# The first shift vector by halves of its columns, worked in between the steps of the first projection

## The chip, the cores and the metric

One Trainium2 chip, of which this kernel uses one core: TensorE (matrix products), VectorE, ScalarE, GpSimd (POOL in the profile) and SyncE (SP), which here does nothing but issue transfers. The metric is device microseconds for one execution, as a median of three runs.

## The reference, cut to what matters

One transformer layer over 256 tokens of 1024 features, batch 1. A condition vector c gives six vectors of 1024, and the first two of them modulate the normalised input ahead of one wide projection:

```
mod = silu(c) @ w_ada + b_ada          # six vectors: sh1, sc1, g1, sh2, sc2, g2
u   = normalize(x) * (1 + sc1) + sh1
proj = u @ w_in                        # 1024 -> 2560: x, y, q, k, v, 512 columns each
mix = [rmsnorm(rg_lru(conv(x)) * gelu(y)), rmsnorm(attention(q, k, v))] @ w_out
x   = layernorm(alpha * x + g1 * mix)
out = layernorm(alpha * x + g2 * experts(modulate(x, sh2, sc2)))   # 32 experts, top 2
```

The change touches only sh1, "the first shift vector", and its way into the first 512 columns (x) of the projection. All weights are float32.

## The kernel before

**Order of work.** The program is written out by hand: each engine executes its instructions in the order of the source, and semaphores hold an instruction until what it reads is there. So an instruction that waits also holds everything behind it on its engine. All large weights are brought by transfers that SP issues in program order (L229 in the helper `load`, two transfers of 1 MB each); a transfer into a buffer is issued once the last reader of the buffer is done.

**Modulation.** The two vectors come from `ada`, the columns of w_ada. `cd` holds silu(c), each value repeated 32 times. `scale_mm(a)` (L361) multiplies it with 512 columns of w_ada for half a of the scale vector: 32 products, each of 128 columns, four of them side by side in the four column strips of the array; float32 takes two instructions for one product, so 64 in the profile. VectorE copies the result out (L368). `scale_end` (L371) turns the row into columns with a small product (L373) and adds the bias on VectorE (L375) into `mod1[:, 1]`. `vec_cols(0)` (L377) does the same for the whole shift vector at once: products of 256 columns (L381), a copy (L384), two small products (L387), and at L465 the bias into `mod1[:, 0]`.

**First projection.** `proj_T` (L419) computes 512 columns of the projection in eight steps k, 12 products (L430) of 256 columns a step. Weights and activations are split into a high and a low float32r part, and three of the four part products are summed. `ahead` (L402) splits the weights: ScalarE writes the high part (L407, or L410 with the scale vector multiplied in), VectorE the low one (L408, L411), into four buffers `w`. `after` is called behind a step's products, `mid` behind the first six.

**The shift in the x part.** The x part runs before the shift vector is known: its weights are multiplied by the scale vector, its activations are the plain normalised input, and the contribution of the shift is one row vector, `shift @ w_in[:, 0:512]`, that is added later as a bias. For it VectorE spreads `mod1[:, 0]` into `shd` (L467), TensorE multiplies `shd` with the x weights (L481, eight products of 512 columns, 16 instructions), ScalarE copies the result (L503), TensorE turns it into columns (L507). All other parts take fully modulated activations, which `u_part(k)` (L469) makes for slice k: ScalarE writes the high part (L470), VectorE (k even) or GpSimd (k odd) overwrites the plain activations (L471), and VectorE subtracts for the low part (L473).

**What stands where.** The x part is L454, with `gate_constants` (L337) behind step 6: a chain of some thirty tiny operations, most of them on GpSimd, each waiting for the one before. Then: issue of the y weights (L455) and of `pkb`; `vec_cols(0)` (L458); the split of the first y weights (L459); issue of the q weights, of `wgt`, of a row of biases behind a GpSimd fill of `brows` (L462), and of the next part of w_ada (L464); the shift vector (L465 to L467); `u_part` 0 and 1; the 16 instructions of L481; issue of the k weights, of T and of another part of w_ada. Then the y part (L515), in whose steps 0 to 5 the `u_part` 2 to 7 stand. Behind it comes one instruction group of `ada_mm` (L578), the q part, and so on through attention, output projection, router and experts.

Of the kernel before, what the change touches and what calls it, by code (L numbers as in the profile page):

```python
# [10 lines left out]
F32 = mybir.dt.float32  # L11
# [4 lines left out]
AF = mybir.ActivationFunctionType  # L16
OP = mybir.AluOpType
# [5 lines left out]
H, DH = 8, 64  # L23
NE, DE = 32, 256
KD = D // 128
# [122 lines left out]
def layer(ctx: ExitStack, tc: tile.TileContext, at_a, at_b, x, w_ada, b_ada, w_in, w_out, w1, w3, w2,  # L148
          pack_a, pack_b, w_gate, rb, ln, out, dbg=None):
    nc = tc.nc  # L150
    te, ve, se, ge, sy = nc.tensor, nc.vector, nc.scalar, nc.gpsimd, nc.sync
# [42 lines left out]
    def bank(pool=None):  # L194
        turn[0] += 1
        return (pool or (psx, psp)[turn[0] % 2]).tile([128, 512], F32, name="b")

    def abank():
        return psa.tile([128, 512], F32, name="a")
# [8 lines left out]
    def A(name):  # L208
        o, w = at_a[name]
        return pka[:, o:o + w]  # L210
# [21 lines left out]
    def load_vec(v, q, s):  # L232
        return load(s, ada[:, 4 * q:4 * q + 4, v * D:(v + 1) * D])

    def load_ada(g, q, s):
        return load(s, ada[:, 2 * q:2 * q + 2, g * 2048:(g + 1) * 2048])

    def load_win(j, s):
        return load(s, win[:, :, j * 512:(j + 1) * 512])
# [13 lines left out]
    for a in range(2):  # L253
        V1[1, a] = load(a, ada[:, :, D + a * 512:D + a * 512 + 512])
        sy.dma_start(W["x"][:, 4 * a:4 * a + 4], win[:, 4 * a:4 * a + 4, 0:512])
    V1[0, 0] = load_vec(0, 0, 3)
    V1[0, 1] = load_vec(0, 1, 4)
    ident = A("ident")

    negh = cst.tile([128, 2], F32, name="negh")  # L260
# [76 lines left out]
    def gate_constants():  # L337

        ge.tensor_scalar(hb, P("ba", 0, 8), 0.5, None, op0=OP.mult)
        lam = P("lam", 0, 4)  # L340
        a_, w_, s_, q_, acc_, r_ = [sp[:, i] for i in range(6)]
        ve.tensor_scalar(a_, lam, -1.0, None, op0=OP.mult)
        ve.tensor_tensor(a_, a_, lam, op=OP.max)
        se.activation(w_, a_, AF.Exp, scale=-1.0)
        ge.tensor_scalar(s_, w_, 2.0, None, op0=OP.add)
        ve.reciprocal(s_, s_)
        ge.tensor_mul(s_, s_, w_)
        ge.tensor_mul(q_, s_, s_)
        ge.memset(acc_, 1.0 / 19)
        for n in range(8, -1, -1):  # L350
            ge.tensor_mul(acc_, acc_, q_)
            ge.tensor_scalar(acc_, acc_, 1.0 / (2 * n + 1), None, op0=OP.add)
        ge.tensor_mul(acc_, acc_, s_)
        ve.tensor_scalar(r_, lam, -1.0, 0.0, op0=OP.mult, op1=OP.max)
        ge.tensor_scalar(acc_, acc_, 2.0, None, op0=OP.mult)
        ge.tensor_add(r_, r_, acc_)
        ge.tensor_scalar(cs[:, 0], r_, -0.5 * LRU_C, None, op0=OP.mult)
        ge.tensor_scalar(cs[:, 1], r_, 0.5 * LRU_C, None, op0=OP.mult)


    def scale_mm(a):  # L361
        pa = abank()
        for k in range(KD):
            for j in range(4):
                te.matmul(pa[32 * j:32 * j + 32, 0:128], cd[:, k], V1[1, a][:, k, j * 128:(j + 1) * 128], start=(k == 0),
                          stop=(k == KD - 1), skip_group_check=True, tile_position=(0, 32 * j))
        r = tmp.tile([128, 256], F32, name="row", bufs=1)[:, 0:128]
        ve.tensor_copy(r, pa[:, 0:128])  # L368
        return r

    def scale_end(a, r):  # L371
        p = bank(psp)
        te.matmul(p[:, 0:4], r, sel4, start=True, stop=True)  # L373
        q = slice(4 * a, 4 * a + 4)
        ve.scalar_tensor_tensor(mod1[:, 1, q], p[:, 0:4], 1.0, A("bcol")[:, 8 + 4 * a:12 + 4 * a], op0=OP.add, op1=OP.add)  # L375

    def vec_cols(v):  # L377
        pa = abank()
        for k in range(KD):
            for j in range(4):  # L380
                te.matmul(pa[32 * j:32 * j + 32, 0:256], cd[:, k], V1[v, k // 4][:, k % 4, j * 256:(j + 1) * 256],  # L381
                          start=(k == 0), stop=(k == KD - 1), skip_group_check=True, tile_position=(0, 32 * j))
        r = tmp.tile([128, 256], F32, name="row", bufs=1)
        ve.tensor_copy(r, pa[:, 0:256])  # L384
        p = bank(psx)
        for s in range(2):
            te.matmul(p[:, s:8:2], r[:, s * 128:(s + 1) * 128], sel4, start=True, stop=True)  # L387
        return p[:, 0:8]

    mod1 = ch.tile([128, 2, 8], F32, name="mod1")  # L390
    for b in range(4):
        n_parts(b)
    scale_end(0, scale_mm(0))
    te.matmul(pv[:H, :384], rbt[:, 384:392], rbt[:, 0:384], start=True, stop=True)


# [2 lines left out]
    def rows_of(w, scale=None):  # L399
        units.extend((w, k, scale) for k in range(KD))  # L400
# [34 lines left out]

    rows_of(W["x"], mod1[:, 1])
    row = [None]

    def after_x(k):
        if k < 2:  # L440
            n_copy(2 * k)
            n_copy(2 * k + 1)
        if k == 1:
            bias_rows()
        if k == 2:
            row[0] = scale_mm(1)
        elif k == 6:
            gate_constants()

    def mid_x(k):  # L450
        if k == 3:
            scale_end(1, row[0])

    px = proj_T(0, psp, after_x, mid_x, lambda k: 4 if k < 4 else 8, (0, 4))  # L454
    W["y"] = load_win(1, 0)  # L455
    sy.dma_start(pkb, pack_b)
    rows_of(W["y"])
    p = vec_cols(0)  # L458
    ahead(9)  # L459
    W["q"] = load_win(2, 3)  # L460
    sy.dma_start(wgt, w_gate)
    ge.memset(brows[:, 0], 0.0)  # L462
    sy.dma_start(brows[0:128:32, 0], b_ada[4:8])
    AD[1, 0] = load_ada(1, 0, 1)  # L464
    ve.tensor_add(mod1[:, 0], p, A("bcol")[:, 0:8])  # L465
    shd = misc[:, 3072:3328].rearrange("p (k n) -> p k n", k=KD)
    ve.tensor_copy(shd, mod1[:, 0, :, None].to_broadcast([128, KD, 32]))  # L467

    def u_part(k):  # L469
        se.activation(ul[:, 0, k], nT[:, k], AF.Identity, scale=mod1[:, 1, k:k + 1], bias=mod1[:, 0, k:k + 1])  # L470
        (ge if k % 2 else ve).tensor_scalar(nT[:, k], nT[:, k], mod1[:, 1, k:k + 1], mod1[:, 0, k:k + 1], op0=OP.mult,  # L471
                                            op1=OP.add)
        ve.tensor_sub(ul[:, 1, k], nT[:, k], ul[:, 0, k])  # L473

    u_part(0)
    u_part(1)

    pb = bank(psx)
    for k in range(KD):
        j = k % 4  # L480
        te.matmul(pb[32 * j:32 * j + 32], shd[:, k], W["x"][:, k], start=(k < 4), stop=(k >= 4), skip_group_check=True,  # L481
                  tile_position=(0, 32 * j))
    W["k"] = load_win(3, 2)
    sy.dma_start(T, bass.AP(tensor=vrd.tensor, offset=vrd.offset, ap=[[1, 128], [384, H], [1, 256]]))
    AD[1, 1] = load_ada(1, 1, 4)
    rowx = brows[:, 1]
    xb = ch.tile([128, 4], F32, name="xb")
    xl, xc = t4(0), t4(1)
# [8 lines left out]
                                    op0=OP.mult, op1=OP.add)  # L497

    def after_y(k):
        if k < 6:  # L500
            u_part(k + 2)
        if k == 0:
            se.activation(rowx, pb, AF.Copy)  # L503
        elif k == 2:
            pb2 = bank(psp)
            for j in range(4):
                te.matmul(pb2[:, j:j + 1], rowx[:, j * 128:(j + 1) * 128], inv32, start=True, stop=True)  # L507
            ve.tensor_copy(xb, pb2[:, 0:4])
        elif k < 7 and k > 2:
            shift(k - 3)  # L510
        if k > 4:
            conv(k - 5)

    rows_of(W["q"])
    py = proj_T(8, psx, after_y)  # L515
    W["v"] = load_win(4, 0)
    gy = nx[:, 1].rearrange("p (m t) -> p m t", m=4)
    for b in range(2):
# [1217 lines left out]
```

## Time and profile before

| | |
|---|---|
| median of 3 runs | 307.26 us (307.08 to 308.35) |
| profiled execution | 307.51 us |
| span of its trace | 305.7 us |
| TensorE busy | 278.0 us, 91% |
| VectorE / ScalarE / GpSimd busy | 181.7 / 108.2 / 23.6 us |
| mean granted TensorE clock | 0.988 of full |
| bytes moved by transfers | 112.22 MB, mean 367 GB/s |

Times are microseconds from the start of the span. The profiled execution took 307.51 us, of which 1.81 us lie around the span. The page gives each engine's busy share in 40 slices, the clock granted to TensorE, and the busy share of the transfer engines; a busy TensorE is not TensorE at its peak, since matrix products overlap. "Chain" is the chain of work that ended last, followed back from the last instruction.

### The profile page before, as it was taken

What the parts mean: (1) busy time and instruction counts of PE and PEld (TensorE: products, weight loads), DVE (VectorE), ACT (ScalarE), POOL (GpSimd) and SP (SyncE); (2) the same over time, 40 slices, a digit from 0 to 9 for tenths busy, and PEclk for the clock granted to TensorE, in tenths of its full rate; (3) what the DMA queues carried; (4) which work ended last, traced back from release to release, by engine and by line L of the source; (5) the groups of instructions that cost most, each with busy time, mean ns of one, the idle gap of its engine ahead of it and who ended that gap; (6) DMA issues with size and microseconds to landing.
All of it is one profiled execution on the core that took longest, in us unless ns stands there. A gap on an engine that the chain in (4) does not pass through costs nothing.

```text
span 305.7 us, 6096 instructions
## 1 busy us (share of the span) xinstructions
PE 278.0 (91%) x2344; PEld 185.1 (61%) x2344; DVE 181.7 (59%) x442; ACT 108.2 (35%) x229; POOL 23.6 (8%) x62
## 2 busy tenths in 40 slices
PE   0699889999999999999988969999999999998980
PEld 0579649797957745457475656667546754664430
DVE  2675167937686796689698964264426343434281
ACT  1233068868937542043417341113111312121110
POOL 0100613000010000000110200000000000400000
PEclk9999979999999999999999999999999999999997
DMA  7999999999999699699969999999999999999404
GB/s 271 387 391 408 393 396 404 385 395 420 411 409 407 248 416 421 235 402 378 323 263 364 364 416 427 418 421 419 423 423 415 421 419 420 421 414 404 177 3 148
DMA packets 26163, 112.22 MB, mean 367 GB/s; under 512 B 2253, under 2 KB 3586, under 8 KB 17420
## 3 DMA queue, kind: packets, MB, share of 16 engines
q1 hardware_dynamic: 25712, 111.26, 91.7%
q10 hardware_dynamic: 348, 0.47, 0.4%
q8 instruction: 20, 0.33, 0.4%
q14 instruction: 19, 0.16, 0.2%
q0 software_dynamic: 64, 0.01, 0.0%
HBM read 110.51 MB, written 1.22 MB: 365 GB/s over the span
## 4 chain that ended last, share of the span: by engine, by line
PE 63%; DMA 13%; DVE 12%; SPq 6%; ACT 2%; issue 2%; DVEq 0%; ACTq 0%
PE m L1212 14%; PE b L430 12%; PE m L1350 8%; PE b L804 7%; DMA arena<-in_w 6%; DMA arena<-in_w_in 6%; SPq L229 4%; PE b L779 4%; PE m L1288 4%; PE acc L1311 3%; PE a L578 2%; PE a L590 2%; PE acc L1387 1%; PE b L481 1%; PE b L617 1%
## 5 line engine op out<-in xcount | busy, mean ns | idle before, releaser
L430 PEld LDWEIGHTS b<-ul,w 128*128 128x128 f32 x384 | 46.6, 192 | 5.0 <-ACT ul L470 1.6
L430 PE MATMUL b<-ul,w 128*128 128x256 f32 x384 | 48.4, 286 | 0.5 <-ACT w L410 0.5
L1212 PE MATMUL m<-arena,xg 128*64 128x256 f32 (+1 forms) x288 | 36.1, 380 | 1.0 <-DMA arena<-in_w 1.0
L408 DVE TENSOR_TENSOR w<-arena,w 128x512 fp32r<-128x512 f32 x32 | 21.9, 700 | 16.1 <-ACT w L407 16.1
L1350 PE MATMUL m<-arena,hT 128*32 128x512 f32 (+2 forms) x184 | 29.1, 596 | 1.6 <-ACT hT L1341 1.6
L804 PE MATMUL b<-arena,mT 128*128 128x512 f32 x64 | 29.0, 601 | 0.0
L1212 PEld LDWEIGHTS m<-arena,xg 128*64 128x64 f32 (+1 forms) x288 | 21.1, 125 | 9.9 <-DMA arena<-in_w 1.7
L407 ACT ACTIVATE w<-arena 128x512 fp32r<-128x512 f32 x32 | 19.5, 625 | 13.9 <-DMA arena<-in_w_in 7.1
L1212 PE MATMUL m<-fifth,xg 128*32 128x256 f32 (+1 forms) x96 | 21.5, 380 | 0.0
L1212 PE MATMUL m<-misc,xg 128*32 128x256 f32 (+1 forms) x160 | 21.4, 380 | 0.0
L1362 DVE SCALAR_TENSOR_TENSOR ys<-m,ws,g2b 128x256 f32<-128x256 f32 (+1 forms) x21 | 11.4, 570 | 16.0 <-PE m L1350 15.8
L1363 ACT ACTIVATE yh<-ys 128x256 fp32r<-128x256 f32 (+1 forms) x21 | 10.0, 488 | 27.0 <-DVE ys L1362 26.9
L1331 DVE TENSOR_TENSOR hh<-hh,m 128x256 f32<-128x256 f32 x7 | 3.0, 422 | 27.9 <-ACT hh L1330 27.9
L804 PEld LDWEIGHTS b<-arena,mT 128*128 128x128 f32 x64 | 11.6, 191 | 13.0 <-issue 12.7
L1350 PEld LDWEIGHTS m<-arena,hT 128*32 128x32 f32 (+2 forms) x184 | 8.6, 120 | 17.8 <-issue 12.7
L1330 ACT ACTIVATE hh<-m 128x256 f32<-128x256 f32 x7 | 2.7, 385 | 41.1 <-PE m L1212 41.1
L1288 PE MATMUL m<-oh,xb 128*128 128x256 f32 (+1 forms) x64 | 15.4, 281 | 1.3 <-DVE oh L1279 1.3
L1288 PE MATMUL m<-oh,xa 128*128 128x256 f32 (+1 forms) x64 | 15.4, 282 | 0.0
L1212 PEld LDWEIGHTS m<-misc,xg 128*32 128x32 f32 (+1 forms) x160 | 13.3, 126 | 1.6 <-issue 0.8
L1212 PE MATMUL m<-last,xg 128*32 128x256 f32 x64 | 14.2, 380 | 0.0
L728 ACT ACTIVATE s<-s,z 128x128 f32<-128x128 f32 (+1 forms) x16 | 7.1, 449 | 18.3 <-DVE z L726 18.3
L305 PE MATMUL b<-pka,nx 128*128 128x128 f32 x16 | 3.9, 428 | 10.3 <-DVE nx L303 10.3
(321 smaller groups left out, 501.2 us busy)
## 6 DMA issues: line engine op xcount, KB each, us to landing
arena<-in_w SPq DMA_DIRECT2D x41, 1024.0 KB, 11.9
arena<-in_w_ada SPq DMA_DIRECT2D x22, 1024.0 KB, 13.9
arena<-in_w_in SPq DMA_DIRECT2D x10, 1024.0 KB, 15.1
last<-in_w SPq DMA_DIRECT2D x6, 1024.0 KB, 12.2
misc<-in_w SPq DMA_DIRECT2D x6, 1024.0 KB, 13.3
fifth<-in_w SPq DMA_DIRECT2D x6, 1024.0 KB, 13.0
arena<-in_w_out SPq DMA_DIRECT2D x4, 1024.0 KB, 8.8
arena<-in_w SPq DMA_DIRECT2D x8, 512.0 KB, 12.7
```

The source lines that it names most:

```text
L229: sy.dma_start(t[:, q], src[:, q])
L407: se.activation(t[:, 0], w[:, k], AF.Copy)
L408: ve.tensor_sub(t[:, 1], w[:, k], t[:, 0])
L430: te.matmul(half(bs, m), t[:, a, m * 128:(m + 1) * 128], ul[:, b, k], start=(k + m % 2 + a + b == 0), stop=(k == KD - 1 and a == 1), skip_ ...
L779: te.matmul(pvv[i], ul[:, ua, k, i * 128:(i + 1) * 128], t[:, wa], start=(k + wa + ua == 0), stop=(k == KD - 1 and wa == 1))
L804: te.matmul(p, mT[:, k, i * 128:(i + 1) * 128], wo[k // 4][:, k % 4, h * 512:(h + 1) * 512], start=(m == 0), stop=(m == 3))
L1212: te.matmul(ph[o:o + w, a * 256:(a + 1) * 256], xs[:, k, o:o + w], place[q][0].rearrange("p (a k f) -> p a k f", a=2, k=KD)[:, a, k], star ...
L1288: te.matmul(q, nhl[i][:, a, k * 128:(k + 1) * 128], oh[:, i, :n], start=(a + i == 0), stop=(a + i == 2))
L1311: te.matmul(acc[i][h], G[:, i * 128:(i + 1) * 128], y[:, sl], start=False, stop=False, skip_group_check=True)
L1350: te.matmul(ps[h][o:o + w], hT[:, j, o:o + w], place[q][1][:, j * 1024 + h * 512:j * 1024 + (h + 1) * 512], start=(j == 0), stop=(j == 1), ...
L1362: ve.scalar_tensor_tensor(ys[:, o:o + q], p[:, o:o + q], ws, g2b[:, sl], op0=OP.mult, op1=OP.mult)
L1363: se.activation(yh[:, sl], ys[:, o:o + q], AF.Copy)
```

## The change

It loads the shift vector's columns of w_ada in two halves of 512 columns, as the scale vector's are, in place of two halves of the rows. `scale_mm` and `scale_end` become `col_mm(v, a)` and `col_end(v, a, r)` for both vectors, and `vec_cols` goes. The first half of the shift vector is worked in the x part: `col_mm(0, 0)` behind step 5, `col_end` and the spread into `shd` in the middle of step 6, `u_part` 0 and 1 behind step 6, 2 and 3 behind step 7. `gate_constants` moves from behind step 6 to behind step 4. The second half stands behind the x part: `col_mm(0, 1)`, then the first half of the shift's product (`shift_mm(0)`), then `col_end` and the spread. The second half of the product stands behind step 0 of the y part, with the issue of the k weights, T and the next w_ada part; `u_part` 4 to 7 stand behind the y steps 0 and 1. Issue of the q weights and what follows is written ahead of `col_mm(0, 1)`. In step 0 of the y part the products with the low weights come last.

```diff
-    V1[0, 0] = load_vec(0, 0, 3)
-    V1[0, 1] = load_vec(0, 1, 4)
+    for a in range(2):
+        V1[0, a] = load(3 + a, ada[:, :, a * 512:a * 512 + 512])
...
-    def scale_mm(a):
+    def col_mm(v, a):
...
-    def scale_end(a, r):
-        p = bank(psp)
+    def col_end(v, a, r):
+        p = bank(psx if v == 0 else psp)
         te.matmul(p[:, 0:4], r, sel4, start=True, stop=True)
         q = slice(4 * a, 4 * a + 4)
-        ve.scalar_tensor_tensor(mod1[:, 1, q], p[:, 0:4], 1.0, A("bcol")[:, 8 + 4 * a:12 + 4 * a], op0=OP.add, op1=OP.add)
+        ve.scalar_tensor_tensor(mod1[:, v, q], p[:, 0:4], float(v), A("bcol")[:, 8 * v + 4 * a:8 * v + 4 * a + 4], op0=OP.add,
+                                op1=OP.add)
...
+    def shift_cols(a):
+        q = slice(4 * a, 4 * a + 4)
+        ve.tensor_copy(shd[:, q], mod1[:, 0, q, None].to_broadcast([128, 4, 32]))
...
         if k == 2:
-            row[0] = scale_mm(1)
+            row[0] = col_mm(1, 1)
+        elif k == 4:
+            gate_constants()
+        elif k == 5:
+            row[0] = col_mm(0, 0)
         elif k == 6:
-            gate_constants()
+            u_part(0)
+            u_part(1)
+        elif k == 7:
+            u_part(2)
+            u_part(3)
 
     def mid_x(k):
         if k == 3:
-            scale_end(1, row[0])
+            col_end(1, 1, row[0])
+        elif k == 6:
+            col_end(0, 0, row[0])
+            shift_cols(0)
...
     W["y"] = load_win(1, 0)
     sy.dma_start(pkb, pack_b)
-    rows_of(W["y"])
-    p = vec_cols(0)
-    ahead(9)
     W["q"] = load_win(2, 3)
     sy.dma_start(wgt, w_gate)
     ge.memset(brows[:, 0], 0.0)
     sy.dma_start(brows[0:128:32, 0], b_ada[4:8])
     AD[1, 0] = load_ada(1, 0, 1)
-    ve.tensor_add(mod1[:, 0], p, A("bcol")[:, 0:8])
-    shd = misc[:, 3072:3328].rearrange("p (k n) -> p k n", k=KD)
-    ve.tensor_copy(shd, mod1[:, 0, :, None].to_broadcast([128, KD, 32]))
...
-    u_part(0)
-    u_part(1)
+    rows_of(W["y"])
+    rows_of(W["q"])
 
     pb = bank(psx)
-    for k in range(KD):
...
+    def shift_mm(a):
+        for j in range(4):
+            te.matmul(pb[32 * j:32 * j + 32], shd[:, 4 * a + j], W["x"][:, 4 * a + j], start=(a == 0), stop=(a == 1),
+                      skip_group_check=True, tile_position=(0, 32 * j))
+
+    r = col_mm(0, 1)
+    shift_mm(0)
+    col_end(0, 1, r)
+    shift_cols(1)
...
     def after_y(k):
-        if k < 6:
-            u_part(k + 2)
+        if k < 2:
+            u_part(2 * k + 4)
+            u_part(2 * k + 5)
         if k == 0:
+            shift_mm(1)
             se.activation(rowx, pb, AF.Copy)
+            W["k"] = load_win(3, 2)
+            sy.dma_start(T, bass.AP(tensor=vrd.tensor, offset=vrd.offset, ap=[[1, 128], [384, H], [1, 256]]))
+            AD[1, 1] = load_ada(1, 1, 4)
...
-    rows_of(W["q"])
-    py = proj_T(8, psx, after_y)
+    py = proj_T(8, psx, after_y, late=(0,))
```

## Rows read from the trace of the kernel before

**Rows 1.** The chain that ended last, 18 to 57 us: start, us, what.
```profile
18.48 18.72 DMA arena<-in_w_in
37.30 0.64 ACT w L407
...
38.58 0.17 DVE mod L465
...
39.12 3.60 PE b L481 x16
42.71 4.50 PE b L430 x36
...
48.00 7.29 PE b L430 x60
55.30 1.85 PE a L578 x16
```
**Rows 2.** Windows, whole stretches: busy by engine (instructions), clock, DMA share, GB/s.
```profile
5.00:20.00 15.00, 8.97 (x97) 7.17 (x98) 9.89 (x22) 4.60 (x9) 1.37 (x3) 1.00 1.05 389
20.00:31.00 11.00, 10.76 (x137) 10.22 (x136) 7.69 (x17) 3.00 (x6) 0.39 (x2) 1.00 1.03 405
43.00:100.00 57.00, 57.00 (x440) 48.06 (x439) 39.44 (x70) 41.05 (x78) 4.07 (x7) 1.00 1.03 404
...
125.00:130.00 5.00, 5.00 (x52) 2.47 (x52) 3.68 (x7) 0.00 (x0) 0.00 (x0) 1.00 0.42 135
```
**Rows 3.** Timeline of GpSimd, 30 to 53 us: start, us, engine, line, operation.
```profile
30.32 0.23 POOL L345 TENSOR_SCALAR sp<-sp 128x4 f32<-128x4 f32 x1 [18.66 <-ACT sp L344]
...
37.92 0.22 POOL L358 TENSOR_SCALAR cs<-sp 128x4 f32<-128x4 f32 x1
38.20 0.52 POOL L462 MEMSET misc<- 128x512 f32 x1
39.97 0.74 POOL L471 TENSOR_SCALAR arena<-arena,mod 128x256 f32<-128x256 f32 x1 [1.25 <-ACT ul L470]
45.65 0.56 POOL L471 TENSOR_SCALAR arena<-arena,mod 128x256 f32<-128x256 f32 x1 [4.94 <-ACT ul L470]
```
**Rows 4.** Timeline of VectorE, 24 to 41 us.
```profile
24.97 0.29 DVE L368 COPY row<-a 128x128 f32<-128x128 f32 x1 [0.96 <-PE a L365]
...
29.63 0.17 DVE L342 TENSOR_SCALAR sp<-pka 128x4 f32<-128x4 f32 x1
...
37.97 0.69 DVE L408 TENSOR_TENSOR w<-arena,w 128x512 fp32r<-128x512 f32 x1 [0.87 <-ACT w L407]
...
39.40 0.41 DVE L471 TENSOR_SCALAR arena<-arena,mod 128x256 f32<-128x256 f32 x1 [0.34 <-ACT ul L470]
39.85 0.42 DVE L473 TENSOR_TENSOR ul<-arena,ul 128x256 fp32r<-128x256 f32 x1
40.73 0.43 DVE L473 TENSOR_TENSOR ul<-arena,ul 128x256 fp32r<-128x256 f32 x1 [0.46 <-POOL arena L471]
```
**Rows 5.** Timeline of TensorE, 22 to 38 us.
```profile
22.95 1.96 PE L365 MATMUL a<-arena,cd 128*32 128x128 f32 x64
...
32.95 3.66 PE L381 MATMUL a<-arena,cd 128*32 128x256 f32 x64
37.15 0.61 PE L387 MATMUL b<-pka,row 128*128 128x4 f32 x4 [0.55 <-DVE row L384]
```
**Rows 6.** Windows of TensorE alone: busy (instructions), granted clock, DMA share, GB/s.
```profile
14.75:15.00 0.25, 0.25 (x12) 1.00 1.03 377
15.50:15.75 0.25, 0.25 (x20) 1.00 1.00 369
...
39.50:42.00 2.50, 2.50 (x16) 0.50 1.04 388
...
42.50:43.00 0.50, 0.50 (x7) 0.97 1.05 389
```
**Rows 7.** Transfers issued by line: count, KB each, median us to landing.
```profile
arena<-in_w_in SPq DMA_DIRECT2D x10, 1024.0 KB, 15.1
```

More of the change, by code (lines that the diff above doesn't have):

```diff
@@ L364, in scale_mm @@
             for j in range(4):
-                te.matmul(pa[32 * j:32 * j + 32, 0:128], cd[:, k], V1[1, a][:, k, j * 128:(j + 1) * 128], start=(k == 0),
+                te.matmul(pa[32 * j:32 * j + 32, 0:128], cd[:, k], V1[v, a][:, k, j * 128:(j + 1) * 128], start=(k == 0),
                           stop=(k == KD - 1), skip_group_check=True, tile_position=(0, 32 * j))
@@ L369, in scale_mm @@
         return r
-    def scale_end(a, r):
-        p = bank(psp)
+    def col_end(v, a, r):
+        p = bank(psx if v == 0 else psp)
         te.matmul(p[:, 0:4], r, sel4, start=True, stop=True)
         q = slice(4 * a, 4 * a + 4)
-        ve.scalar_tensor_tensor(mod1[:, 1, q], p[:, 0:4], 1.0, A("bcol")[:, 8 + 4 * a:12 + 4 * a], op0=OP.add, op1=OP.add)
-    def vec_cols(v):
-        pa = abank()
-        for k in range(KD):
[L380 to L388, printed above, removed]
+        ve.scalar_tensor_tensor(mod1[:, v, q], p[:, 0:4], float(v), A("bcol")[:, 8 * v + 4 * a:8 * v + 4 * a + 4], op0=OP.add,
+                                op1=OP.add)
     mod1 = ch.tile([128, 2, 8], F32, name="mod1")
@@ L392, in layer @@
         n_parts(b)
-    scale_end(0, scale_mm(0))
+    col_end(1, 0, col_mm(1, 0))
     te.matmul(pv[:H, :384], rbt[:, 384:392], rbt[:, 0:384], start=True, stop=True)
@@ L437, in layer, with u_part @@
     row = [None]
+    shd = misc[:, 3072:3328].rearrange("p (k n) -> p k n", k=KD)
+    def shift_cols(a):
+        q = slice(4 * a, 4 * a + 4)
+        ve.tensor_copy(shd[:, q], mod1[:, 0, q, None].to_broadcast([128, 4, 32]))
+    def u_part(k):
+        se.activation(ul[:, 0, k], nT[:, k], AF.Identity, scale=mod1[:, 1, k:k + 1], bias=mod1[:, 0, k:k + 1])
+        (ge if k % 2 else ve).tensor_scalar(nT[:, k], nT[:, k], mod1[:, 1, k:k + 1], mod1[:, 0, k:k + 1], op0=OP.mult,
+                                            op1=OP.add)
+        ve.tensor_sub(ul[:, 1, k], nT[:, k], ul[:, 0, k])
     def after_x(k):
@@ L464, in layer @@
     AD[1, 0] = load_ada(1, 0, 1)
-    ve.tensor_add(mod1[:, 0], p, A("bcol")[:, 0:8])
-    shd = misc[:, 3072:3328].rearrange("p (k n) -> p k n", k=KD)
-    ve.tensor_copy(shd, mod1[:, 0, :, None].to_broadcast([128, KD, 32]))
[L469 to L473, printed above, removed]
-    u_part(0)
-    u_part(1)
-    pb = bank(psx)
[L479 to L485, printed above, removed]
+    rows_of(W["y"])
+    rows_of(W["q"])
+    pb = bank(psx)
+    def shift_mm(a):
[6 more added lines that the diff above has]
+    shift_cols(1)
     rowx = brows[:, 1]
```

## The prediction

> **What bounds the kernel now.** I read the chain of waits first, then windows, then the timelines of the engines around 30 to 45 us. The chain shows that between 18 and 39 us the kernel waits for the y weights, which land at 37.2; then come their split, the shift vector's bias and spread, the 16 instructions of L481, and from 42.71 nothing but TensorE [rows 1]. TensorE is busy without a gap from 43 to 100 us, and so are the transfer engines (share 1.03); later there are stretches in which these run dry, 0.42 at 125 to 130 us, while TensorE is full [rows 2]: they wait for buffers that TensorE sets free. So TensorE's position at about 44 us decides, and I price a shift there one to one into the end. The mark is the start of the second y step: 42.71 + 4.50 / 3 = 44.2 us before [rows 1].
>
> Two things in this stretch are easily missed. GpSimd runs the gate constants from 30.32 to 38.14, one tiny operation after another [rows 3]. And TensorE's granted clock is half between 39.1 and 42.5 us [rows 6], after a stretch from 36.61 to 39.12 in which it did only the 0.61 us of L387 [rows 5]: L481 takes 3.60 us, where L578, also 16 instructions of 512 columns, takes 1.85 [rows 1].
>
> **The change, part by part.**
>
> *Moved into the x part.* The 64 instructions of L381 (3.66 us) become two groups of 64 with half the columns, 1.96 us each by L365 [rows 5]; the four small products of L387 (0.61) become two pairs of 0.30. The x part ended at 32.95 [rows 5]; with one group and one pair in it, 35.2. The transfers for it are the first in their order as before, and L381 ran straight behind the x part, over both halves, without a break, so both halves are there in time. The second group then ends at 37.2, and the first half of L481's work, 8 instructions, costs half of 1.85, 0.93: TensorE is through at 38.1. What it needs next is the small product of the second half, and that needs VectorE's copy.
>
> *The moved `gate_constants`.* Written two steps earlier, it starts when it did: its first VectorE operation ran at 29.63 with no wait ahead of it [rows 4], directly behind the low splits of the last x weights, and these stand ahead of it in the new order too. So I cost the move at nothing, and GpSimd's chain still ends at 37.92 + 0.22 = 38.14 [rows 3].
>
> *The added wait.* `u_part(1)` and `u_part(3)` have an operation on GpSimd, and in the new order it stands behind that chain, while VectorE's subtraction that reads it stands ahead of the copy of the second half. Queued behind this subtraction on VectorE are `u_part(2)`, the subtraction of `u_part(3)`, the copy, the bias, the spread, and the low split of the y weights; TensorE waits for the copy. From the rows [rows 3, 4], with some 0.05 us between two operations: GpSimd's operation starts at 38.20, where the fill of `brows` started, and takes 0.56 to 0.74, done at 38.76 to 38.95; then subtraction 0.43, L471 0.41, subtraction 0.42, subtraction 0.43 (GpSimd's second operation is hidden behind these), copy 0.29: 40.8 to 41.0. With the small pair, 0.30, TensorE goes on at 41.2. Bias 0.17 [rows 1], spread about 0.2 (an estimate, a little over half of the 0.30 us between L465's end and L481's start), low split 0.69 [rows 4]: 42.4. The old cover was that VectorE had nothing to do while GpSimd worked on the constants; it is gone, and its price is 41.2 less 38.1, about 3 us of TensorE.
>
> *The y part.* Step 0 starts with eight products that need only high weights (the y weights, at 37.30 plus 0.64 [rows 1], are long split): at 7.29 / 60 = 0.12 each, 1.0 us, to 42.2; the four others wait for the low split until 42.4 and end at 42.9. The second half of L481's work, another 0.93, stands behind step 0: the second step starts at 43.8, against 44.2. At full clock the change is thus worth 0.1 to 0.4 us; I take 0.3.
>
> *The clock.* TensorE has its pause now from 38.1 to 41.2 but for 0.3 us, 2.8 us idle, against 1.9 us (36.61 to 39.12 less 0.61) before which the clock fell [rows 5, 6]. The row gives no other pause of this length with a full clock behind it. So I take it that the clock falls again, from about the resumption, for as long as before (3.4 us). Step 0 then takes 2.9 us (41.2 to 44.1; the wait for the split is inside), the first 0.5 us of the second half of L481's work runs at half pace, the rest at full, to 45.3. That is 1.1 us later than before. If it doesn't fall, the 0.3 us gain stands: the bounds are -0.4 and, with the fall placed a step later, +1.4.
>
> *Transfers and queues.* The shift columns come in rows half as long, as the scale columns did: 389 GB/s from 5 to 20 us against 405 from 20 to 31 [rows 2]. For 4.19 MB that is 10.78 against 10.36 us, so the y weights land up to 0.4 us later; TensorE waits till 41.2 in any case, so nothing. On SP the q weights are issued some 2 us earlier, when the first group's read of their buffer is done. The bias row waits for the fill of `brows`, which now stands behind GpSimd's two operations: 39.5 to 40.0 in place of 38.20 [rows 3]; the next w_ada part behind it is 1.3 us later, and the k weights, T and another part move behind step 0, to 44 or 45. The order is unchanged, and a weight transfer takes 15.1 us from issue to landing [rows 7], so the engines have work throughout; the first to be used is the w_ada part, at 55.30 [rows 1], 14 us after its issue. I cost this at nothing; without that cover it would be at most the 3 to 4 us of the late issue.
>
> *A rule against the change.* The row: GpSimd's operation took 0.74 us where VectorE's subtraction ran beside it at its start, and 0.56 elsewhere [rows 3, 4]. The Trainium skill says, in "SBUF — State Buffer", section "Who interferes with whom", that VectorE with two operands from SBUF and GpSimd share a pair of ports, and that whoever comes second stands still until the other is through. By that rule, the first subtraction would stand still for all of GpSimd's operation for `u_part(3)`, which starts at the same moment, and everything would be 0.5 us later, 308.9; by the row it is 0.2. It stays inside the forecast's own range.
>
> **The sum.** TensorE's second y step 1.1 us later. The profiled execution took 307.51 us, 1.81 of it outside the span, so that one would become 308.6; it is 0.25 above the median, against which I forecast 307.26 + 1.1 = **308.4 us**, own range 307.8 to 309.1.
>
> **The rivals.**
>
> *Stall, but full clock* (0.24): the pause is split between other work and does not cost the clock. For it: a pause of 1.35 us alone stands before the fall in the rows' strictest reading, and I don't know what the fall hangs on; against it: the new pause is longer than the old one. 307.26 - 0.3 = 307.0, range 306.6 to 307.4.
>
> *The stall does not come* (0.14): the constants or the operations behind them let VectorE through, so that the copy runs at 37.3 and TensorE does not pause. Then step 0 starts at 38.3, is done at 39.8, the half product at 40.7: 3.5 us before 44.2, so 303.8. For it: the whole old path from 37.97 to 42.71 [rows 1] would be gone, and nothing else in the trace is late there. Against it: GpSimd's rows, which leave no gap to slip into. The point from which it decides is GpSimd's end of the constants before about 34 us.
>
> *The half clock lasts longer* (0.12), the slower end: the same stall, but the clock comes back late, as at the start of the kernel, where TensorE began at about 10 us and ran 12 of the small products in a quarter of a microsecond until 15.0, and 20 from 15.5 on [rows 6], over 5 us. With 5.4 us at half pace, step 0 and the half product take 4.8 us, to 46.0, and 0.3 us more is lost in the next step: 2.1 us, 309.4. It decides from a half-clock stretch of some 4.5 us.
>
> *Absorbed* (0.06): the shift is given back at 125 to 130 us, where transfers have room: 307.3.
>
> **How the numbers follow.** The forecast has 0.44. Half a per cent, 1.54 us, is about what a measurement of this kernel can tell from no change: 305.7 to 308.8. Of the forecast's 0.44, 0.29 lie below 308.8 and 0.15 above, by the rule on ports or a late fall of the clock. Same: 0.29 + 0.24 + 0.06 = 0.59; slower: 0.15 + 0.12 = 0.27; faster: 0.14. The range leaves out the case without stall and the end of the long half clock, 0.18 together: 305.8 to 309.8.
>
> **What would show it.** In the changed profile: GpSimd's constants end at 38.1, followed by its two operations for `u_part`; VectorE idle from about 35 to 38.8 with GpSimd as releaser; TensorE idle from 38.1 to about 41; granted clock 0.50 in the microseconds after it; the second y step at 45.3 (43.8 at full clock). Wrong would be: VectorE's copy of the second half before 39 us, a full clock behind the pause, or a start of the q part that moves by another amount than the end of the kernel.

## The result, and the profile after

The changed kernel took 311.87 us (median of six executions, 308.22 to 312.96), the kernel before 308.06 on the same chip: a ratio of 1.0103 [1.0062, 1.0145]. Run again on another chip, twelve times, it took 309.66 us against 307.77, 1.006 [1.0019, 1.0101]. The ratios leave out executions of more than 1.5% above the fastest of the same kernel (one of these six, two of these twelve, and elsewhere a few, of up to 1576 us), so the quotient of two medians can be larger. The changed kernel is thus slower, by 0.6 to 1%, on the side that the forecast named but further out: 1.1 us was forecast, and the ratios are worth 3.2 and 1.8 us; 308.4 was forecast, and the range ended at 309.8. The profiled execution took 308.22 us, of which 306.4 are its span.

The chain that ended last, 37 to 48 us, of the kernel after (start, us, what). Before, it went from the y weights over ScalarE to TensorE [rows 1]; now the chain of GpSimd's gate constants, which begins at 28.8 us, runs straight into it, and VectorE and TensorE follow. Line numbers are those of each kernel: in the changed one L418 are the products of `proj_T` (L430 before), L479 those of the shift (L481), L373 the small product, L368 the copy ahead of it, L433, L434 and L436 the three operations of `u_part` (L470, L471, L473), L395 ScalarE's split (L407) and L582 `ada_mm` (L578); in the kernels of the experiments they move by a few lines.

```profile
37.17 0.22 POOL cs L358
...
37.49 0.56 POOL arena L434
38.08 0.43 DVE ul L436
...
40.26 0.21 DVE row L368
40.52 0.59 PE b L373 x2
...
44.88 3.06 PE b L418 x24
```

The timelines of VectorE, GpSimd, ScalarE and TensorE of the kernel after, with the idle time before an instruction and what ended it in brackets. They answer to [rows 3 to 5].

```profile
38.08 0.43 DVE L436 TENSOR_TENSOR ul<-arena,ul 128x256 fp32r<-128x256 f32 x1 [4.30 <-POOL arena L434]
38.42 1.04 DVE L434 TENSOR_SCALAR arena<-arena,mod 128x256 f32<-128x256 f32 x1
39.50 0.76 DVE L436 TENSOR_TENSOR ul<-arena,ul 128x256 fp32r<-128x256 f32 x2
40.18 0.28 DVE L368 COPY row<-a 128x128 f32<-128x128 f32 x1
...
37.49 1.36 POOL L434 TENSOR_SCALAR arena<-arena,mod 128x256 f32<-128x256 f32 x2
...
37.85 2.19 ACT L395 ACTIVATE w<-arena 128x512 fp32r<-128x512 f32 x4 [3.50 <-DMA arena<-in_w_in]
...
34.22 1.96 PE L365 MATMUL a<-arena,cd 128*32 128x128 f32 x64
35.99 1.04 PE L479 MATMUL b<-arena,misc 128*32 128x512 f32 x8
40.52 0.59 PE L373 MATMUL b<-pka,row 128*128 128x4 f32 x2 [3.48 <-DVE row L368]
40.97 2.91 PE L418 MATMUL b<-ul,w 128*128 128x256 f32 x12
43.80 1.07 PE L479 MATMUL b<-arena,misc 128*32 128x512 f32 x8
44.80 1.45 PE L418 MATMUL b<-ul,w 128*128 128x256 f32 x10
```

VectorE stands still for 4.30 us until the first GpSimd operation for `u_part` is done, and that stands behind the constants. The copy of the second half could have been made from 36.2 on, when the products that it reads were done; it starts at 40.18. TensorE pauses for 3.48 us, although the weights that come next are split from 37.85 on. TensorE alone in windows (busy, instructions, granted clock, share and GB/s of the transfers), which answers to [rows 6]:

```profile
36.00:37.03 1.03, 1.03 (x16) 1.00 1.05 388
37.03:40.50 3.47, 0.01 (x1) 0.99 1.04 394
40.50:43.75 3.25, 3.23 (x14) 0.50 1.05 389
```

The clock is at its lower level from the end of the pause on, for 3.4 us. The mark of the prediction, the second y step, stands at 44.80 here, 0.6 us later than before, and the span is 0.7 us longer.

### The profile page after: what moved, and what is told of

Same layout as the page of the kernel before. It is cut to its first block, busy times and chain, and to the rows that moved or that the text cites. A ratio compares the mean times of both kernels' runs of the same rounds, so it can differ in the third digit from the quotient of the medians.

```text
span 306.4 us, 6232 instructions
## 1 busy us (share of the span) xinstructions
PE 277.1 (90%) x2408; PEld 186.8 (61%) x2408; DVE 182.6 (60%) x445; ACT 108.3 (35%) x229; POOL 25.1 (8%) x62
## 4 chain that ended last, share of the span: by engine, by line
PE 66%; DVE 17%; DMA 8%; ACT 3%; POOL 3%; issue 2%; DVEq 0%; ACTq 0%; POOLq 0%
PE m L1216 14%; PE b L418 14%; PE m L1354 8%; PE b L808 7%; DMA arena<-in_w 6%; PE b L783 4%; PE m L1292 4%; PE acc L1315 3%; PE a L582 2%; PE a L594 2%; DMA pka<-in_pack_a 1%; PE acc L1391 1%; PE b L621 1%; DVE arena L1413 1%; DVE w L399 1%
## 5 line engine op out<-in xcount | busy, mean ns | idle before, releaser
L418 PE MATMUL b<-ul,w 128*128 128x256 f32 x384 | 50.3, 290 | 0.5 <-ACT w L398 0.5
L418 PEld LDWEIGHTS b<-ul,w 128*128 128x128 f32 x384 | 48.0, 196 | 4.4 <-ACT w L398 1.4
L395 ACT ACTIVATE w<-arena 128x512 fp32r<-128x512 f32 x32 | 19.4, 625 | 9.8 <-PE b L418 5.8
L1334 ACT ACTIVATE hh<-m 128x256 f32<-128x256 f32 x7 | 2.7, 384 | 41.1 <-PE m L1216 41.1
L1216 PEld LDWEIGHTS m<-fifth,xg 128*32 128x32 f32 (+1 forms) x96 | 11.1, 119 | 3.5 <-issue 1.4
```

What stands on the lines that cost most here:

```text
L395: se.activation(t[:, 0], w[:, k], AF.Copy)
L418: te.matmul(half(bs, m), t[:, a, m * 128:(m + 1) * 128], ul[:, b, k], start=(k + m % 2 + a + b == 0), stop=(k == KD - 1 and a == 1), skip_ ...
L1216: te.matmul(ph[o:o + w, a * 256:(a + 1) * 256], xs[:, k, o:o + w], place[q][0].rearrange("p (a k f) -> p a k f", a=2, k=KD)[:, a, k], star ...
```

## The experiments

Each ratio is against the kernel before on the same chip. Where a number of microseconds at half clock is given for an execution that left no trace, it is worked out as twice the span times what the mean granted clock lacks to full.

**The theories.** A: VectorE's wait behind GpSimd, with the pause and the half clock that follow, costs the time. B: the transfers do, by half rows and later issues.

**The changed kernel again.**

> The changed kernel once more, to see how its executions spread. Theory A (VectorE held behind GpSimd makes TensorE pause, and the pause costs granted clock; the number of half-clock stretches differs between executions): mean granted clocks fall into groups, about 0.989 near 308, 0.984 near 310 to 311, 0.979 near 312 to 313, and each group lies 1.5 to 2 us above the next better one; median 310 to 312. Theory B (the loss lies in transfers: shorter rows, later issues): time does not follow the clock.

It took 309.66 us, a little less than the 310 to 312 expected, and the groups are loose: executions with a mean clock of 0.991 took 307.36 to 309.58 us, those with 0.988 took 309.54 to 311.73, those with 0.979 took 311.29 and 312.92. The second y step of its trace stood at 46.12. More traces of this kernel stand further down.

**Three ways to take the wait away.** In the first, VectorE does the two operations that stand behind the constants:

```diff
-        (ge if k % 2 else ve).tensor_scalar(nT[:, k], ...
+        (ge if k > 3 and k % 2 else ve).tensor_scalar(nT[:, k], ...
```

> One edit on the changed kernel: u_part 1 and 3 use VectorE in place of GpSimd, so nothing stands behind the gate constants. Theory A: VectorE's copy of the second half at about 37.3 us, no pause of TensorE above 1 us, clock full in 30 to 60 us, second y step at 40.5 to 41.0, 3.5 us ahead of the kernel before: 303.5 to 305. Theory B: like the changed kernel, 310 to 312.

306.13 us, 0.9923 [0.9896, 0.9949]; the second y step at 41.32, and a wait of 1.21 us for the split of the y weights. In the second the constants come behind y step 2:

```diff
-        elif k == 4:
-            gate_constants()
...
         elif k == 2:
+            gate_constants()
```

> The other way to take the wait away: the gate constants move behind step 2 of the y part, u_part 1 and 3 stay on GpSimd. Theory A: as with all on VectorE, 303.5 to 305, second y step at 40.5 to 41.2. Theory B: 310 to 312.

305.74 us, 0.9946 [0.9908, 0.9984], the second y step at 41.86. Both are on the side of theory A and both miss its size, 303.5 to 305 us, by 1.1 and 0.7 us. In the third they come behind step 0 of the x part, where GpSimd and VectorE have room:

```diff
+        if k == 0:
+            gate_constants()
...
-        elif k == 4:
-            gate_constants()
```

> The third way to take the wait away: the gate constants behind step 0 of the x part, so that GpSimd is through with them by about 31 us, ahead of u_part 1; everything else as changed. Theory A: as with u_part 1 and 3 on VectorE, 305.5 to 306.5, the y part's first step at 38.7 to 39.0, set by the landing of the y weights. Theory B: 309.7 to 311.9.

305.52 us, 0.995 [0.9926, 0.9975], as expected; GpSimd was through with the constants at 32.60 (31 expected), and the y part's first step began at 38.35. **And one to make it longer**: the constants behind step 6, still ahead of `u_part`.

```diff
-        elif k == 4:
-            gate_constants()
...
         elif k == 6:
+            gate_constants()
             u_part(0)
```

> The changed kernel with the gate constants behind step 6 of the x part, ahead of u_part 0: the wait made longer. They start some 4 us later, so GpSimd is through at 41 to 42 in place of 37.4 to 38.5. Theory A: VectorE's copy at about 44, the y part's first step 3 to 4 us later than in the changed kernel, and the end with it: 313 to 315.5. Theory B (transfers): as the changed kernel, 309.7 to 311.9.

312.84 us, 1.0208 [1.0165, 1.0251], a little under what was expected. TensorE's timeline of the third of the cures:

```profile
37.12 1.04 PE L479 MATMUL b<-arena,misc 128*32 128x512 f32 x8
38.10 0.39 PE L373 MATMUL b<-pka,row 128*128 128x4 f32 x2
38.35 1.98 PE L418 MATMUL b<-ul,w 128*128 128x256 f32 x12
40.26 1.07 PE L479 MATMUL b<-arena,misc 128*32 128x512 f32 x8
41.26 3.14 PE L418 MATMUL b<-ul,w 128*128 128x256 f32 x24
```

And of the kernel with the longer wait:

```profile
36.42 1.04 PE L478 MATMUL b<-arena,misc 128*32 128x512 f32 x8
44.48 0.59 PE L373 MATMUL b<-pka,row 128*128 128x4 f32 x2 [7.01 <-DVE row L368]
44.92 2.91 PE L418 MATMUL b<-ul,w 128*128 128x256 f32 x12
47.76 1.13 PE L478 MATMUL b<-arena,misc 128*32 128x512 f32 x8
48.82 1.34 PE L418 MATMUL b<-ul,w 128*128 128x256 f32 x9
```

There is no pause in the one and twice the pause in the other, and the second y step is at 41.26 and at 48.82. The transfers and their order are the same in all of these kernels. The time of their issue is not quite: the bias row, which SP issues behind GpSimd's fill of `brows`, goes out at 39.34 in the changed kernel, at 38.53 in the third cure and at 43.31 in the kernel with the longer wait, and the next part of w_ada behind it. But from 36 to 110 us TensorE waits for no transfer in the changed kernel or in the one with the longer wait; the only wait of TensorE that the traces list there is the one for VectorE's copy. So B falls as the cause of the loss at the mark, and A is shown, from both sides. Against the mark the medians lie nearly on a line: 305.5 to 306.1 us at 41.3 to 41.9 (the cures), 309.7 at 45.5 (mean of eight traces, below), 312.8 at 48.8. From the cures to the longest wait that is 7.0 us at the end for 7.3 at the mark, so the price of one for one was nearly right.

**The pause without the clock.** 22 spare products, whose results nobody reads, fill TensorE's pause in the changed kernel:

```diff
+        for _ in range(fill):
+            te.matmul(p[:, 256:512], ul[:, 0, 7, 0:128], ul[:, 0, 7], start=True, stop=True, skip_group_check=True)
         te.matmul(p[:, 0:4], r, sel4, start=True, stop=True)
...
-    col_end(0, 1, r)
+    col_end(0, 1, r, 22)
```

> The wait stays, but TensorE gets 22 spare products of 256 columns (2.7 us at full clock, results unused) in the pause ahead of the second half's small product. Theory A: granted clock stays full, second y step at 43.8 to 44.3, 306.5 to 307.5, so that of the loss against the changed kernel's 311 some 4 us are clock and the rest is the pause itself. Rival C (pause alone, the clock costs nothing at the end): no faster than the changed kernel, 311 or more. Theory B: 311.

308.82 us, 1.0033 [0.9998, 1.0067]. TensorE in its trace:

```profile
37.72 2.89 PE L374 MATMUL b<-ul 128*128 128x256 f32 x22
41.28 0.39 PE L375 MATMUL b<-pka,row 128*128 128x4 f32 x2 [0.67 <-DVE row L368]
41.53 2.00 PE L420 MATMUL b<-ul,w 128*128 128x256 f32 x12
43.45 1.06 PE L481 MATMUL b<-arena,misc 128*32 128x512 f32 x8
44.45 3.14 PE L420 MATMUL b<-ul,w 128*128 128x256 f32 x24
```

The twelve products of step 0 take 2.00 us in place of 2.91, so the clock stays up here. By the medians that is worth 0.8 us (309.66 less 308.82), and the wait alone costs the other 2.7 (308.82 less 306.13). The order of the two was expected the other way round, some 4 us for the clock and 306.5 to 307.5 us for this run: a miss. The 0.8 us are not firm, since the intervals of the two ratios overlap; at the mark it is 44.45 against 45.5. The 2.7 us are clear of noise.

**The same in the kernel before**, whose own pause was followed by half a clock in the profiled execution [rows 5, 6]: 4 spare products ahead of L387 and 9 behind it.

```diff
+        for _ in range(4):
+            te.matmul(p[:, 256:512], ul[:, 0, 7, 0:128], ul[:, 0, 7], start=True, stop=True, skip_group_check=True)
         for s in range(2):
             te.matmul(p[:, s:8:2], r[:, s * 128:(s + 1) * 128], sel4, start=True, stop=True)
+        for _ in range(9):
+            te.matmul(p[:, 256:512], ul[:, 0, 7, 0:128], ul[:, 0, 7], start=True, stop=True, skip_group_check=True)
```

> The kernel before with 13 spare products of TensorE (1.6 us, results unused) in its pause between L381 and L481, so that its clock should not fall there. Theory A (the kernel before loses about 1.75 us to the clock on the shift's 16 products in many of its executions, so a sound price for the change has to be made at equal clock): 306.0 to 306.6, mean granted clock 0.992 or more. Rival D (the y weights' landing alone sets the start of the y part, the clock is hidden): no change, 307.5 to 308.

A miss: 307.27 us, 1.0 [0.9973, 1.0027]. Its timeline:

```profile
39.74 1.92 PE L485 MATMUL b<-arena,misc 128*32 128x512 f32 x16 [0.59 <-DVE misc L471]
41.60 4.58 PE L434 MATMUL b<-ul,w 128*128 128x256 f32 x36
```

The clock is full (1.92 in place of 3.60), the y part starts 1.1 us earlier than before, and the spare products themselves held the path up for some 0.6 us; yet the median doesn't move. The trace shows where this execution gives the gain back: it is still 1.0 us ahead at 181.42 us (182.43 before), and then waits longer for an expert's weights. The kernel before and this one:

```profile
277.07 0.40 PE L1212 MATMUL m<-arena,xg 128*32 128x256 f32 x1 [1.04 <-DMA arena<-in_w]
276.83 0.40 PE L1216 MATMUL m<-arena,xg 128*32 128x256 f32 x1 [1.79 <-DMA arena<-in_w]
```

That wait is 0.8 to 1.9 us in every trace but that of look 3 (below), so one execution with 1.79 says little. The executions without a trace point to the other reason: of the kernel before, 21 of 35 on this chip had less than 5 us at half clock anyway, with a median of 306.5 us; here it is 9 of 12, with 307.2. The spare products cost about as much as they save.

**Half rows alone.** The kernel before with only the shift vector's columns brought in two halves:

```diff
-    V1[0, 0] = load_vec(0, 0, 3)
-    V1[0, 1] = load_vec(0, 1, 4)
+    for a in range(2):
+        V1[0, a] = load(3 + a, ada[:, :, a * 512:a * 512 + 512])
...
-                te.matmul(pa[32 * j:32 * j + 32, 0:256], cd[:, k], V1[v, k // 4][:, k % 4, j * 256:(j + 1) * 256],
+                te.matmul(pa[32 * j:32 * j + 32, 0:256], cd[:, k], V1[v, j // 2][:, k, (j % 2) * 256:(j % 2) * 256 + 256],
```

> The kernel before with one part of the change alone: the shift vector's columns come in two halves of 512 columns (rows half as long), everything else as it was. As predicted the y weights land 0.4 us or more later (traces with the change show 37.85 to 38.0 for ScalarE's first split, against 37.30); here nothing hides it: 0.4 to 0.8 us above the kernel before, 308.2 to 308.6. Rival: no difference, 307.8.

A miss as well: 306.40 us, 0.9981 [0.9955, 1.0008]. The expected delay is in the trace (the y weights at 38.18, TensorE waits 0.66 us for the second half), but it doesn't reach the end in the median. Nor does it when like is compared with like: the executions with at most 4.3 us at half clock took 306.2 us (the kernel before 306.5), the others 307.8 (307.7). A median of so mixed a set also jumps with the share of the two groups.

```profile
35.41 1.92 PE L381 MATMUL a<-arena,cd 128*32 128x256 f32 x28 [0.66 <-DMA arena<-in_w_ada]
```

**An earlier start at full clock.** 90 spare products from the first microsecond on, in both kernels:

```diff
     pv = bank(psp)
+    for _ in range(90):
+        te.matmul(pv[:, 0:128], oneb, oneb, start=True, stop=True)
```

> The kernel before with the same 90 spare products. Theory E: the y weights' landing hides the start of TensorE, no change: 307.4 to 308.0. Rival: the start reaches the end here too: 306 to 307.

307.88 us, 1.0021 [0.9987, 1.0054], as expected.

> The changed kernel with 90 spare bfloat16 products on TensorE from about 1 us, so that its clock is full by the first real product. Theory E (new): behind the change the y part hangs on GpSimd's constants, and these on the x part, so what the slow clock costs the first products (up to 1.7 us, different from execution to execution) now reaches the end: 307.3 to 308.5, 1 to 2 us below the changed kernel, with less spread. Rival F (the start is hidden by transfers in both kernels): as the changed kernel, 309.7 to 312.

310.22 us, 1.0073 [1.0032, 1.0115], a miss: the spare products were through at 7.6 us, and in the thin work behind them the clock fell again. It doesn't test what it was made for. But it shows that what the rival "the half clock lasts longer" assumed can happen: behind the same pause of 3.48 us, half the clock lasts from 41.4 to 48.2 us (windows of TensorE alone):

```profile
41.00:44.00 3.00, 1.71 (x8) 0.56 1.03 380
44.00:48.00 4.00, 4.00 (x18) 0.50 1.07 412
```

**A better version?** The first and the third cure, each with the second half of the shift's product and the issues behind it moved ahead of the y part (`shift_mm(1)`, the k weights, T, w_ada).

> u_part 1 and 3 on VectorE, and the second half of the shift's product ahead of the y part, into the time in which TensorE waits there for the y weights (1.2 us). Second y step 0.6 to 0.8 us earlier than without it (41.3), so 305.2 to 305.9 against 306.1.

> The gate constants behind step 0 of the x part, u_part 1 and 3 on GpSimd as in the change, and the second half of the shift's product ahead of the y part. As the version on VectorE or slightly better, since VectorE is free earlier: 305.0 to 305.8.

305.76 us, 0.9958 [0.9932, 0.9983], and 305.49, 0.9951 [0.9928, 0.9974]: within what was expected, but no better than the cures alone. In the first the second y step stands at 41.5, not earlier than without it. In the second, the y part starts at 38.95 and the second step at 40.5, but 14 us later TensorE waits for the part of w_ada:

```profile
51.54 1.06 PE L582 MATMUL a<-arena,cd 128*32 128x512 f32 x8
53.61 1.06 PE L582 MATMUL a<-arena,cd 128*32 128x512 f32 x8 [1.00 <-DMA arena<-in_w_ada]
```

The earlier work meets a transfer that doesn't land earlier. Half a per cent below the kernel before, in the first cure 0.8%, is what this rearrangement gives without the wait.

**Where the long executions lose.** Five of the first six executions of the changed kernel have 9.9 to 13.7 us at half clock, of which the stretch behind the pause explains 3.4 and the end of the kernel, where TensorE is thinly used, 1.7 to 4.0 more (in the traces). Six more executions were traced one by one to show the rest; they are called looks 1 to 6, as in the expectations.

> The changed kernel, one execution with its trace. If the clock theory holds, its span is 304.4 to 306.4 us plus half a microsecond for each microsecond at half clock, and the half-clock stretches beyond the one behind the pause lie where TensorE has pauses: behind the pause itself, as a second stretch that follows at once, or at the router near 166 us. If the rival holds (the long executions are slower transfers), the clock is full there and the start of the second y step is late with TensorE waiting for weights.

> As the look before it: the changed kernel, another execution. Time 306 to 308 us with 5.5 to 6.7 us at half clock, 311 to 313 with 10 to 13; in a long one the extra stretches follow the pause at about 41 us or the router at 166 us.

> As the two looks before it, a third execution of the changed kernel. The start of the second y step lies at 44.8 to 46.1 us where only one stretch of 3.4 us follows the pause, at about 47.4 where two do, and the end of the span moves with it by the same amount, but for a stretch at the router, which costs the end by itself.

> The changed kernel, a fourth look. By the clock theory with late transfers: an execution of 311 us or more has, beside the half-clock stretch behind the pause, one or two more of 3.4 us, each directly behind a wait of TensorE for an expert's weights that is 1 us or more longer than the 0.8 to 1.1 us of the other traces, as the third look had near 280 us. By the rival: the extra stretches stand behind the pause or at the router, without a late transfer.

> As the fourth look, another execution of the changed kernel: 307.6 to 309.4 us with 5.5 to 7.4 us at half clock and no late transfer, or 311 to 313 us with 9.9 to 13.7 us at half clock and at least one late transfer among the experts' weights.

> As the fourth and the fifth look. In each of the three the second y step starts at 44.8 to 46.2 us, and a half-clock stretch of 3.4 us lies behind the pause.

All eight traces of the changed kernel, with the times of one execution each; the last column is the span less the second y step:

| trace | time | GpSimd's constants end | second y step | rest |
|---|---|---|---|---|
| first | 308.22 | 37.39 | 44.80 | 261.6 |
| again | 309.38 | 38.47 | 46.12 | 261.5 |
| look 1 | 309.09 | 38.19 | 45.80 | 261.5 |
| look 2 | 307.64 | 37.38 | 44.85 | 261.1 |
| look 3 | 312.17 | 37.49 | 44.96 | 265.4 |
| look 4 | 310.62 | 38.63 | 46.18 | 262.6 |
| look 5 | 310.86 | 38.71 | 46.35 | 262.7 |
| look 6 | 309.26 | 37.66 | 45.07 | 262.4 |
| mean | 309.66 | 38.0 | 45.5 | 262.3 |
| before | 307.51 | 38.14 | 44.2 | 261.5 |

A half-clock stretch of 3.4 us lies behind the pause in all eight. The third look has another: TensorE waits 2.95 us for an expert's weights, where the other seven wait 0.8 to 1.9, and behind it the clock is half again. Its timeline of TensorE:

```profile
278.12 0.62 PE L1216 MATMUL m<-arena,xg 128*32 128x256 f32 x2 [1.07 <-DMA arena<-in_w]
280.62 0.63 PE L1216 MATMUL m<-arena,xg 128*32 128x256 f32 x1 [1.88 <-DMA arena<-in_w]
```

Its windows of TensorE alone:

```profile
277.00:279.75 2.75, 0.67 (x4) 1.00 1.00 399
279.75:283.25 3.50, 2.63 (x28) 0.51 1.03 400
```

The fourth has one at the router, where TensorE is thinly used in all traces; the fifth, with the same work, doesn't. Windows of the fourth look:

```profile
163.00:166.00 3.00, 1.11 (x6) 1.00 0.94 336
166.00:169.75 3.75, 3.75 (x10) 0.54 0.93 367
```

And of the fifth:

```profile
163.00:166.00 3.00, 1.13 (x6) 1.00 0.87 311
166.00:169.75 3.75, 3.75 (x24) 1.00 0.97 365
```

So an extra stretch occurs at the router, as the first looks expected, and behind a late transfer, as the third showed and the fourth was to confirm; none followed the first stretch at once. A late transfer without any half clock (look 5 and 6, 1.88 us of waiting) makes the rest longer too. Three expectations are missed in part: the third look's extra stretch was at neither of the two places named for it, the fourth's stood without a late transfer, and the fifth, at 310.86 us with 6.4 us at half clock, fits neither branch, with its second y step, at 46.35, a little beyond the range as well. No execution with 13 us at half clock was caught.

## Why the prediction was wrong, point by point

**The wait: right.** The chain ends as foreseen, the two operations follow it, VectorE was held from 33.8 to 38.08 by GpSimd, and TensorE went on at 40.52 (forecast 41.2) for want of the copy. Counted from the end of the constants, the copy came 3.07 us later; the prediction's sum is 2.7 to 2.9. The difference stands where GpSimd works beside: VectorE's first two operations took from 38.08 to 39.48 beside GpSimd's second, 1.4 us, against 0.43 + 0.04 + 0.41 alone. That is 0.5 us, the amount that the prediction gave for the rule of the Trainium skill ("SBUF — State Buffer", "Who interferes with whom"), where it took 0.2 from the row. The trace agrees with that rule in the amount only: the subtraction, with two operands from SBUF, kept its 0.43 us, and the operation behind it was stretched, from 0.41 to 1.04.

**The half clock: right in length, and nearly in place.** It follows the pause in all eight traces, for 3.4 us, beginning within 0.3 us of the resumption in four of them and 1.0 to 1.6 us behind it in the others, and the mean of the second y step is 45.5 us, where 45.3 was forecast.

**The moved constants at nothing: right in the mean, but with a spread that was left out.** "GpSimd's chain still ends at 37.92 + 0.22 = 38.14" took a place from one execution as fixed. The eight traces have 38.0 in the mean. In the table the second y step follows the constants' end by 7.4 to 7.7 us in every trace, and that end varies by 1.3 us, since the chain starts behind the x weights' splits and these behind TensorE's first products. These differ between executions: between 15.00 and 15.25 us TensorE ran 20 of the small products of L365 in the first trace and 12 in the fifth look, and the product of L373 behind them starts at 16.05 and at 17.35. The granted clock is 1.00 in both, so the rows don't show what slows them. A window and a line of TensorE's timeline of the first trace:

```profile
15.00:15.25 0.25, 0.25 (x20) 1.00 1.05 385
16.05 0.39 PE L373 MATMUL b<-pka,row 128*128 128x4 f32 x2 [0.55 <-DVE row L368]
```

And of the fifth look:

```profile
15.00:15.25 0.25, 0.25 (x12) 1.00 1.05 385
17.35 0.39 PE L373 MATMUL b<-pka,row 128*128 128x4 f32 x2 [0.42 <-DVE row L368]
```

Before, TensorE's slack ahead of the y weights took this up; now GpSimd's chain is on the path and hands it to the end.

**The sum: the step that failed.** "TensorE's second y step 1.1 us later. The profiled execution took 307.51 us [...] so that one would become 308.6", set against the median. The mark itself is nearly right: 1.3 us later in the mean of the eight traces, where 1.1 was forecast. What failed is the mark from which the loss was counted, and the rest that was taken as fixed.

First, 44.2 is the mark of one execution that had itself lost 3.4 us to half the clock. With the 16 products of L481 at full clock (1.92 us, as with the 13 spare products, and not 3.60) it would be 42.5, an estimate from these two rows, and the changed kernel's 45.5 would be 3.0 later. The kernel before doesn't always lose: of thirty executions beside the second run of the changed kernel (the one of 417 us left out), thirteen have 3.0 to 4.9 us at half clock and took 306.4 us in the median. The end of the kernel alone has 1.6 to 4.4 us in the traces, and no trace with a stretch of 3.4 us has less than 5.0 in all, so most of the thirteen can't have had the stretch. On the two other chips it is 21 of 35 and 19 of 29. Of 24 executions of the changed kernel one has so little (4.9). Against such a mixture the loss at the mark lies between 1.3 and 3.0 us, not at 1.1. "At full clock the change is worth 0.1 to 0.4 us" likewise compares 43.8 at full clock with 44.2 at half; with the clock kept full behind the pause, the changed kernel took 308.82, not the 307.0 of that rival.

Second, all that follows was taken as unchanged, 261.5 us; the traces of the changed kernel have 261.1 to 265.4, 262.3 in the mean, by late weights and by half-clock stretches further on. That is 0.8 us unpriced: the eight traces are 2.15 us longer in the mean than the one before. How much of the 0.8 us belongs to the change is open, since the kernel before has one trace only, and its variant with the 13 spare products has 262.8 us there. The first run of the changed kernel, 3.2 us slower by its ratio, lies above what the mark explains; five of its six executions have the extra half clock.

**The transfers: nearly right.** The y weights are split from 37.85 on (37.30 before), 0.55 us later where up to 0.4 was allowed, and 387 GB/s at 20 to 31 us stand against 405 [rows 2]. Under the wait this costs nothing, as said. Without it, it is what ends the next wait: in the first cure TensorE waits 1.21 us for the split of these weights.

**The rivals.** "The stall does not come" had 303.8 us; with the constants out of the way it is 305.5 to 306.1, and the second y step at 41.3, not at 40.7. Its condition, an end of the constants well before 34 us, is what the third cure makes true (32.60). "Absorbed" falls: a shift at 44 us comes through almost whole, 7.0 us of 7.3. "The half clock lasts longer" was the nearest in time, but for another reason than it gave: in the traces of the changed kernel the extra half clock lies elsewhere than behind the pause. Nor is the start of the kernel an example of it, as that rival has it: the rows named there have 12 and 20 products at a granted clock of 1.00 alike [rows 6].

**Open.** Eleven of the 24 executions of the changed kernel have over 9 us at half clock, two of those thirty of the kernel before, none of the 64 on the two other chips, and none of the cures' (at most 6.7). Why later stretches come so much oftener behind this wait, and where the second one lies in executions with 13 us, isn't settled. Nor is the difference between the two runs of the same kernel, 1.0103 and 1.006, whose intervals overlap.

## What to carry to other kernels

Before moving work of one engine behind another's serial chain of tiny operations, look where that chain ends and who stands in program order behind the one that waits for it; put such a chain where its engine has room, or give the few operations behind it to another engine: both turned a loss of 0.6 to 1% into a gain of 0.5 to 0.8%. A sum of microseconds from one profiled execution needs the same clock on both sides: ask whether the execution of before has already paid for the loss that you add, and how many of its other executions have. And a wait that goes into the path also carries the spread of whatever starts its chain.

## What the runs showed of the hardware

Behind TensorE's pause of 3.5 us the clock fell in all eight traces, to half, and stayed there for 3.4 us, with TensorE at work again; the fall came between the resumption and 1.6 us after it. Behind the same pause it was half for 6.8 us in the kernel with the early spare products, of which 5.9 us with TensorE at work; with a pause of 7.0 us it was half for 6.8 us too, from 41.1 us on, 3.4 of them inside the pause. It stayed up where 22 spare products left only 0.67 us of the pause. Where TensorE's work is thin, at the router, the same work is followed by half a clock in one execution and by the full clock in another. One stretch of 3.4 us costs up to 1.7 us, as L481's 3.60 us against 1.92 show, and the time of an execution goes with its half-clock time. But not all of the spread is clock: look 5 took 310.86 us with 6.4 us at half clock, look 2 307.64 us with 5.3.

VectorE's operation of L434, 0.41 us alone, took 1.04 us while GpSimd worked on a slice of the same size, and GpSimd's took 0.81 in place of 0.55; the subtraction ahead of it, beside the same GpSimd operation, kept its 0.43.
